# The second layer's modulation sums, divided between the context feed-forward and the first latent feed-forward

## The chip, the cores and the metric

One core of a Trainium2 chip runs the whole program. The time is the device time of one execution in microseconds; the profile is one further execution of the same program, recorded by the hardware profiler. TensorE does matrix products, VectorE, ScalarE and GpSimd the rest, and SyncE issues transfers between HBM and SBUF; each engine works through its own queue in order.

## The reference

A transformer of two layers with width 1024 works on 1024 latent tokens `x` and 256 context tokens `ctx`, in fp32. The first layer mixes by recurrences, the second by attention; both end in a gated feed-forward with a convolution over three tokens. Each layer has six modulation vectors (`_ada`), for the latent tokens from the condition `c` and for the context tokens from `c_ctx`.

```python
def _rms(x):
    xf = x.astype(jnp.float32)
    return (xf * lax.rsqrt(jnp.mean(xf * xf, axis=-1, keepdims=True) + EPS)).astype(x.dtype)

def _modulate(h, shift, scale):
    return h * (1.0 + scale) + shift

def _ada(cond, w, b):
    m = (jax.nn.silu(cond) @ w + b)[:, None, :]
    return jnp.split(m, 6, axis=-1)

def _conv_ffn(h, w_up, conv_w, w_down):
    gate, val = jnp.split(h @ w_up, 2, axis=-1)
    gate = _dwconv(gate, conv_w)
    return (jax.nn.silu(gate) * val) @ w_down

    for i in range(DEPTH):
        last = i == DEPTH - 1
        ml = _ada(c, mod_w[i], mod_b[i])
        mc = _ada(c_ctx[None], mod_w[i], mod_b[i])
        h_l = _modulate(_rms(x), ml[0], ml[1])
        h_c = _modulate(_rms(ctx), mc[0], mc[1])
        ...
        x = x + ml[2] * mix_l
        x = x + ml[5] * _conv_ffn(_modulate(_rms(x), ml[3], ml[4]), ffn_w_up[i], ffn_conv[i], ffn_w_down[i])
        if not last:
            ctx = ctx + mc[2] * mix_c
            ctx = ctx + mc[5] * _conv_ffn(_modulate(_rms(ctx), mc[3], mc[4]), ffn_w_up[i], ffn_conv[i], ffn_w_down[i])
    return _rms(x) * final_norm
```

In the attention of the second layer, queries and keys are normalised by `_rms` over their 128 channels, multiplied by a gain and, for latent tokens, rotated.

## The kernel before

The stages follow each other in this order in the span: recurrences (to about 940 us), output projection of the recurrent mixer (to 1117), feed-forward of the context tokens (`ffn_ctx`, to 1400), feed-forward of the latent tokens in the first layer (`ffn_run(0, ...)`, to about 2070), queries, keys and values of the second layer (to about 2300), attention, the second layer's latent feed-forward (`ffn_run(1, ...)`), the last normalisation. The program is written stage by stage, with generators that mix work of one stage into another; a scheduler that runs when the program is built then fixes the order of the instructions on every engine from its own estimate of times. A tile pool with so many buffers limits how far a load can run ahead of its use.

**Modulation sums.** `mod_steps` computes one part of a modulation vector. For each of 8 blocks of 128 rows of `mod_w` it loads a tile `mw`, and VectorE adds `mw` times a scalar per partition to `macc` (`ts` for the first, L98, `stt` for the others, L103). Then TensorE sums `macc` over the partitions (`mps`, L229), and VectorE adds the bias (`mod<-mps,modb`). For the second layer (l = 1) all six indices are worked on in the context stage, in pieces of 512 columns with two `mw` buffers: 12 pieces x 8 = 96 loads of 256 KB, asked for with `next(mods)` five times per hidden block f, on SyncE's queue. Indices 0 and 1 are needed for both conditions (`macc0`, `macc1`), the others for the latent tokens alone.

**Context stage.** `ffn_ctx` goes over NF = 22 hidden blocks of 128 channels. `up_mm` multiplies with fp32 weights (`fg<-hx,st`, L1203, 256 tokens wide), and after every four blocks `downs` adds to `xT[0]` (`fd<-ft,st`, L1212). Weights come in tiles `st` of 256 KB on the same queue. Beside it `ffn_prep` normalises the latent tokens for the next stage, in 8 pieces of 128 tokens (`rm_ps`: two matmuls a piece, L173 and L180, with a power on GpSimd between them, `rm_cs`). At the end the context tokens are normalised and modulated for the second layer and written to `x0_scr`.

**Latent stage.** `ffn_run` goes over the same 22 blocks. `up(f)` loads 512 KB of weights twice, splits them into a high and a low part (ScalarE copies, GpSimd or VectorE subtracts: `w0h`, `w0l`, `s0h`, ...) and multiplies three times (`mm3`, L155 to L157), in a scheme that needs seven products instead of eight (`u`, `fraw`, `p` are its sums; `st<-st` are sums of weights). `silu_conv` forms the gate on `ft`, and `gated` splits the result into `gh` and `gl`. After every two blocks `downs` multiplies with the down weights (`dh`, `dl`, loads `sd` of 128 KB) into `fd`, and VectorE adds to `xT`. Pools here: `wd` (4 buffers), `g` (2), `st` (2), `w` (1), `t` (1).

**Norm and rope.** `norm_rope` in the stage of queries, keys and values squares (`qsq`, ScalarE), sums (`qss`, VectorE), takes the power (`qrs`, GpSimd), multiplies (`qn`, VectorE) and rotates.

Of the kernel before, what the change touches and what calls it, by code (L numbers as in the profile page):

```python
# [70 lines left out]
def kernel(  # L71
# [139 lines left out]
    def mod_steps(pool, psp, tag, l, idx, conds, part, width, bufs=2):  # L211
# [13 lines left out]
        for d in conds:  # L225
            ps = psp.tile([128, 512], F32, tag=tag, name="mps")
            w_ = 128 if width < 512 else 1
            for m in range(nm):
                T.matmul(ps[:, m * w_:m * w_ + w_], lhsT=acc[d][:, m * 128:(m + 1) * 128], rhs=ones[:, 0:w_],  # L229
                         start=True, stop=True)  # L230
            j0 = c0 // 128
            m_ = modc[l][d][:, j0:j0 + nm]
            tt(V, m_, ps[:, 0:nm * w_].rearrange("p (m n) -> p m n", n=w_)[:, :, 0:1].rearrange("p m n -> p (m n)"),
               modb[:, l * 48 + j0:l * 48 + j0 + nm], ALU.add)
            if idx in (1, 4):
                ts(V, m_, m_, 1.0, None, ALU.add)
            if idx == 5:
                ts(V, m_, m_, 0.5, None, ALU.mult)
# [213 lines left out]
    eG = const.tile([128, NB, 8], F32, name="eG")  # L452
    nG = const.tile([128, NB, 8], F32, name="nG")
    eT = const.tile([128, NB, 8], F32, name="eT")
    ekc = const.tile([128, NB, 8], F32, name="ekc")
    rq2 = const.tile([128, 4, NB], F32, name="rq2")
    rqs = const.tile([128, 4, NB], F32, name="rqs")
# [1176 lines left out]
```

## Time and profile before

| | |
|---|---|
| median of 3 runs (lowest, highest) | 3442.43 us (3440.96, 3444.37) |
| profiled execution: time, span | 3442.76 us, 3441.0 us |
| mean granted TensorE clock | 0.962 |
| busy: TensorE, VectorE | 3195.9 us (93%), 2402.4 us (70%) |
| busy: GpSimd, ScalarE | 1436.7 us (42%), 1278.5 us (37%) |
| moved by DMA | 350.10 MB, mean 102 GB/s |

The span goes from the first to the last instruction; the time of the execution has 1.76 us around it. Shares of busy time are averages over stages with different limits, so single stages are read from windows, waits and timelines below.

### The profile page before, as it was taken

How to read it: one execution, taken by the hardware profiler on the slowest of the kernel's cores; microseconds unless marked ns; L12 is line 12 of the kernel's file. 1: busy time of each engine (PE TensorE's matmuls, PEld its weight loads, DVE VectorE, ACT ScalarE, POOL GpSimd, SP SyncE). 2: the span in 40 equal slices, each digit the busy share in tenths (PEclk: the TensorE clock that was granted, in tenths of full speed). 3: DMA queues.
4: the chain of work that ended last, by engine and by line, in shares of the span. 5: the costliest groups of instructions: out<-in, count | busy, mean ns of one | idle time of the engine just before them, and what ended most of it. 6: DMA issues, size and time to landing. Idle time of an engine off the chain costs nothing.

```text
span 3441.0 us, 47011 instructions
## 1 busy us (share of the span) xinstructions
PE 3195.9 (93%) x16708; PEld 2666.6 (77%) x16708; DVE 2402.4 (70%) x4108; ACT 1278.5 (37%) x2772; POOL 1436.7 (42%) x1269
## 2 busy tenths in 40 slices
PE   7987988999979998899999997999999799999998
PEld 4776877777768887778788786988888678887877
DVE  5567467568777866676777768677567767777677
ACT  4434233653321212333333333346556433333333
POOL 2232231233214111465565553753433655655554
PEclk9998999999989999899999998999999899999999
DMA  5445444655586677212111111330111111111111
GB/s 185 117 117 164 134 133 130 180 152 163 185 263 187 195 231 213 71 52 59 49 55 44 52 57 51 112 99 32 44 47 31 32 53 52 55 45 52 58 50 71
DMA packets 439241, 350.10 MB, mean 102 GB/s; under 512 B 55989, under 2 KB 379807, under 8 KB 438239
## 3 DMA queue, kind: packets, MB, share of 16 engines
q1 hardware_dynamic: 439006, 347.10, 34.0%
q8 instruction: 132, 2.16, 0.3%
q14 instruction: 103, 0.84, 0.1%
HBM read 286.25 MB, written 60.76 MB: 101 GB/s over the span
## 4 chain that ended last, share of the span: by engine, by line
PE 44%; DVE 7%; POOL 3%; issue 2%; ACT 2%; DMA 0%; DVEq 0%; POOLq 0%; ACTq 0%
PE fg L157 6%; PE fg L155 6%; PE fg L156 6%; PE fd L156 4%; PE fd L157 4%; PE fd L155 4%; PE apo L155 2%; PE apo L157 2%; PE apo L156 2%; DVE st L94 2%; PE apt L1512 2%; POOL w1l L94 1%; PE s L155 1%; PE qps L157 1%; PE qps L156 1%
## 5 line engine op out<-in xcount | busy, mean ns | idle before, releaser
L103 DVE SCALAR_TENSOR_TENSOR xT<-fd,mod,xT 128x512 f32<-128x512 f32 (+1 forms) x432 | 290.9, 694 | 193.8 <-PE fd L157 174.0
L155 PE MATMUL pj<-hhi,whi 128*128 128x512 f32 (+1 forms) x696 | 263.8, 379 | 21.3 <-ACT raw L510 14.7
L156 PE MATMUL fd<-gl,dh 128*128 128x512 f32 (+1 forms) x688 | 267.8, 389 | 6.7 <-DVE gl L94 6.6
L157 PE MATMUL fd<-gh,dl 128*128 128x512 f32 (+1 forms) x688 | 266.8, 388 | 0.0
L155 PE MATMUL fd<-gh,dh 128*128 128x512 f32 (+1 forms) x688 | 262.6, 392 | 1.0 <-ACT gh L1140 0.7
L156 PE MATMUL pj<-hlo,whi 128*128 128x512 f32 (+1 forms) x696 | 261.0, 375 | 1.2 <-DVE hlo L94 1.2
L157 PE MATMUL pj<-hhi,wlo 128*128 128x512 f32 (+1 forms) x696 | 259.7, 373 | 0.0
L94 DVE TENSOR_TENSOR st<-st 128x512 f32<-128x512 f32 x176 | 211.6, 1203 | 48.7 <-POOL s1l L94 35.6
L103 DVE SCALAR_TENSOR_TENSOR macc<-mw,sc,macc 128x512 f32<-128x512 f32 (+2 forms) x210 | 177.4, 873 | 82.4 <-DMA mw<-in_mod_w_dram 81.4
L94 POOL TENSOR_TENSOR dl<-sd,dh 128x256 fp32r<-128x256 f32 x168 | 156.1, 944 | 107.4 <-ACT dh L160 107.4
L100 POOL TENSOR_SCALAR P<-P,rc 128x512 f32<-128x512 f32 (+1 forms) x192 | 116.2, 622 | 199.3 <-DVE rc L1498 64.1
L94 POOL TENSOR_TENSOR wlo<-wst,whi 128x512 fp32r<-128x512 f32 x58 | 77.4, 1336 | 271.0 <-ACT whi L160 270.7
L94 POOL TENSOR_TENSOR w0l<-st,w0h 128x1024 fp32r<-128x1024 f32 x44 | 106.0, 2410 | 189.5 <-ACT w0h L1085 134.9
L155 PEld LDWEIGHTS pj<-hhi,whi 128*128 128x128 f32 x696 | 138.3, 199 | 45.9 <-ACT raw L510 17.0
L1203 PE MATMUL fg<-hx,st 128*128 128x256 f32 x704 | 168.5, 393 | 4.3 <-DMA st<-in_ffn_w_up_dram 3.6
L156 PEld LDWEIGHTS fd<-gl,dh 128*128 128x128 f32 x688 | 130.0, 189 | 39.3 <-DVE gl L94 12.8
L94 POOL TENSOR_TENSOR p<-p,u 128x512 f32<-128x512 f32 (+1 forms) x45 | 94.2, 2094 | 149.6 <-DVE u L94 149.6
L103 DVE SCALAR_TENSOR_TENSOR ft<-fraw,conv_f,ft 128x1024 f32<-128x1024 f32 x88 | 135.6, 1541 | 29.2 <-ACT ft L91 28.4
L155 PEld LDWEIGHTS fd<-gh,dh 128*128 128x128 f32 x688 | 128.1, 188 | 35.4 <-ACT gh L1140 9.9
L1203 PEld LDWEIGHTS fg<-hx,st 128*128 128x128 f32 x704 | 136.2, 197 | 24.7 <-DMA st<-in_ffn_w_up_dram 2.1
L156 PEld LDWEIGHTS pj<-hlo,whi 128*128 128x128 f32 x696 | 138.3, 199 | 19.5 <-DVE hlo L94 1.4
L157 PEld LDWEIGHTS pj<-hhi,wlo 128*128 128x128 f32 x696 | 138.0, 198 | 18.9 <-issue 0.2
(609 smaller groups left out, 9697.5 us busy)
## 6 DMA issues: line engine op xcount, KB each, us to landing
st<-in_ffn_w_up_dram SPq DMA_DIRECT2D x88, 512.0 KB
mw<-in_mod_w_dram SPq DMA_DIRECT2D x96, 256.0 KB
st<-in_ffn_w_up_dram SPq DMA_DIRECT2D x88, 256.0 KB
sd<-in_ffn_w_down_dram SPq DMA_DIRECT2D x176, 128.0 KB
sh<-sh_scr SPq DMA_DIRECT2D x80, 256.0 KB
wst<-in_rec_w_in_dram SPq DMA_DIRECT2D x56, 256.0 KB
st<-in_rec_w_out_dram SPq DMA_DIRECT2D x24, 512.0 KB
mw<-in_mod_w_dram SPq DMA_DIRECT2D x24, 512.0 KB
```

The source lines that it names most:

```text
L94: e.tensor_tensor(out=o, in0=a, in1=b, op=op)
L100: e.tensor_scalar(out=o, in0=a, scalar1=s1, scalar2=s2, op0=op0, op1=op1)
L103: e.scalar_tensor_tensor(out=o, in0=a, scalar=s, in1=b, op0=op0, op1=op1)
L155: T.matmul(ps, lhsT=wh, rhs=xh, start=first, stop=False)
L156: T.matmul(ps, lhsT=wh, rhs=xl, start=False, stop=False)
L157: T.matmul(ps, lhsT=wl, rhs=xh, start=False, stop=last)
L1203: T.matmul(ps, lhsT=h[k // 4][:, k % 4], rhs=hx[:, k], start=k == 0, stop=k == KD - 1)
L1512: T.transpose(pt_[:, b], P[:, (b0 + b) * 128:(b0 + b + 1) * 128], ident)
```

## The change

The sums of the second layer are divided. Indices 1, 0 and 2 stay in the context stage, now in pieces of 256 columns, loaded by GpSimd's queue into six buffers; `mod_chain` puts the end of a piece (`fin`: matmuls on `macc` and the addition of the bias) two steps into the next piece, and `fill` is called within `ffn_ctx` at the places where weights are loaded. Indices 4, 3 and 5 move into the first latent feed-forward, in pieces of 256 columns on SyncE's queue with two buffers, by `fill` in `ffn_run`.

Buffers change places: some small tables lie in a pool on the right side that is closed after the recurrences; the latent stage's pools `st`, `w` and `t` lie on the right and are opened before the context tokens' last normalisation; that normalisation (`ctx_out`) becomes a hook after `up(0)` of the latent stage; `wd` gets three buffers instead of four, and the last block's down weights go into the tiles `s0` and `s1`; `fsta` has 11 buffers instead of 12.

In `norm_rope` the sum of squares is taken by ScalarE itself (`accum_out`), and the product `qn` moves from VectorE to ScalarE.

```diff
+    pa = ExitStack()
+    rcs = pool(pa, "rcs", 1, side="right")
...
+    def mod_steps(pool, psp, tag, l, idx, conds, part, width, bufs=2, eng=None, late=None):
...
-        acc = {d: pool.tile([128, width], F32, tag=f"macc{d}", name="macc") for d in conds}
+        acc = {d: pool.tile([128, width], F32, tag=f"macc{d}", name="macc", bufs=1 if late is None else 2) for d in conds}
...
-            dma(w, mod_w[l, k * 128:(k + 1) * 128, c0:c0 + width])
+            (eng or nc.sync).dma_start(out=w, in_=mod_w[l, k * 128:(k + 1) * 128, c0:c0 + width])
...
+    def mod_chain(specs):
+        late = []
+        for sp in specs:
+            for i, _ in enumerate(mod_steps(*sp, late=late)):
+                if i == 1 and len(late) > 0:
+                    late.pop(0)()
+                yield
+        for fin in late:
+            fin()
...
-    def ffn_run(l, p, ops, early):
+    def ffn_run(l, p, ops, early, hook=None, fill=lambda: None):
...
                 for ci in (1, 2):
                     for k in (kp, kp + 1):
                         down(fs, hs, k, ci, 0, 512)
+                    fill()
...
             t1 = up(f)
+            if f == 0 and hook is not None:
+                hook()
...
             gated(f, t1)
-        w1 = [w_part(f, kp) for kp in range(0, KD, 2)]
+            fill()
+        if l == 0:
+            w1 = []
+            for e in range(2):
+                big = hilo(p.w, [128, 4, 128], f"s{e}")
+                w1 += [w_part(f, 4 * e + kp, [u[:, kp:kp + 2] for u in big]) for kp in (0, 2)]
+        else:
+            w1 = [w_part(f, kp) for kp in range(0, KD, 2)]
...
                 h = [weight(w_down(0, f), hf) for f in fs]
+                fill()
...
             pg = up_mm(w_up(0, f * 128))
             if f % GRP_F == 0 and f:
                 downs(range(f - GRP_F, f))
+            fill()
             pv_ = up_mm(w_up(0, DFF + f * 128))
+            fill()
...
-            mods = (None for i in (1, 0, 2, 4, 3, 5) for h in range(2)
-                    for _ in mod_steps(mp, pd, "d", 1, i, (0, 1) if i < 2 else (0,), h, 512))
+            mods = mod_chain([(mp, pd, "d", 1, i, (0, 1) if i < 2 else (0,), q, 256, 6, nc.gpsimd) for i in (1, 0, 2) for q in range(4)])
...
-                for _ in range(5):
-                    next(mods, None)
+                next(mods, None)
+                next(mods, None)
...
-            hx = hilo(h0, [128, KD, NCTX], "m0")
-            rms_mod(tmp, pd, "d", xT[0], NCTX, mcol(1, 1, 1), mcol(1, 1, 0), *hx, w=128)
-            for i in range(2):
-                dma(x0_scr[i], hx[i])
-    with ExitStack() as pf:
-        p = Ffn()
-        ffn_pools(p, 0, pf, (("wd", 4), ("g", 2), ("st", 2), ("w", 1), ("t", 1)))
-        ffn_run(0, p, ops, 0)
+        h0s.close()
+    pf = ExitStack()
+    p = Ffn()
+    x0p = pool(p0, "x0p", 1)
+    for nm, b in (("st", 2), ("w", 1), ("t", 1)):
+        setattr(p, nm, pool(pf, f"f{nm}0", b, side="right"))
+
+    def ctx_out():
+        for o in range(0, NCTX, 128):
+            xs = xT[0][:, :, o:o + 128]
+            rb, sq = normalised(x0p, pd, "d", xs)
+            tt(V, sq, xs, rb, ALU.mult)
+            scale_shift(sq, sq, mcol(1, 1, 1), mcol(1, 1, 0))
+            hi = x0p.tile([128, KD, 128], F32R, tag="xhi", name="xhi")
+            lo = sq.bitcast(F32R)
+            for k in (0, 4):
+                S.copy(out=hi[:, k:k + 4], in_=sq[:, k:k + 4])
+                tt(V, lo[:, k:k + 4], sq[:, k:k + 4], hi[:, k:k + 4].bitcast(F32), ALU.subtract)
+            dma(x0_scr[0][:, :, o:o + 128], hi)
+            dma(x0_scr[1][:, :, o:o + 128], lo)
+        p0.close()
+        p.wd = pool(pw, "fwd0", 3)
+        p.g = pool(pw, "fg0", 2)
+        mq.append(pool(pw, "fm0", 1))
+
+    with ExitStack() as pw:
+        mq = []
+        mods = mod_chain([(mq, pd, "d", 1, i, (0,), q, 256) for i in (4, 3, 5) for q in range(4)])
+        ffn_run(0, p, ops, 0, ctx_out, lambda: next(mods, None))
...
             def norm_rope(ps, b, a):
                 sq = qt_.tile([128, 2, 128], F32, tag="sq", name="qsq")
-                act(sq, ps, AF.Square)
-                ss = qt_.tile([128, 2], F32, tag="ss", name="qss")
-                V.tensor_reduce(out=ss, in_=sq, axis=AX.X, op=ALU.add)
...
+                for h in range(2):
+                    S.activation(out=sq[:, h], in_=ps[:, h], func=AF.Square, accum_out=ss[:, 0, h:h + 1])
...
-                tt(V, qn, ps, rs[:, :, None].to_broadcast([128, 2, 128]), ALU.mult)
+                for h in range(2):
+                    act(qn[:, h], ps[:, h], AF.Copy, scale=ss[:, 1, h:h + 1])
```

The scheduler's order shows how the instructions move. The first place is GpSimd's queue at the start of the context stage, before the change; `wol` are the last splits of the output projection's weights, and `rm_cs` is the power on which TensorE's `rm_ps` waits.

```order
L94 TENSOR_TENSOR wol<-st,woh 128x1024 x13
L176 TENSOR_TENSOR rm_cs<-rm_cs,nhalf 128x1 x2
L94 TENSOR_TENSOR wol<-st,woh 128x1024
L100 TENSOR_SCALAR hx<-rm_sq,mod_72 128x128 x4
L94 TENSOR_TENSOR wol<-st,woh 128x1024 x2
L176 TENSOR_TENSOR rm_cs<-rm_cs,nhalf 128x1
L100 TENSOR_SCALAR rm_sq<-rm_sq,mod_71 128x128 x2
```

The same place in GpSimd's queue after the change, from the last two `wol` on:

```order
L94 TENSOR_TENSOR wol<-st,woh 128x1024 x2
L221 DMA mw<-in_mod_w_dram 128x256 x22
L178 TENSOR_TENSOR rm_cs<-rm_cs,nhalf 128x1
L100 TENSOR_SCALAR rm_sq<-rm_sq,mod_74 128x128 x2
L221 DMA mw<-in_mod_w_dram 128x256
L178 TENSOR_TENSOR rm_cs<-rm_cs,nhalf 128x1
L221 DMA mw<-in_mod_w_dram 128x256 x7
L100 TENSOR_SCALAR rm_sq<-rm_sq,mod_74 128x128 x2
```

The loads of `mw` have come into this queue, in runs of up to 22 ahead of a power. The second place is TensorE's queue where the context stage (`fd` from `ft` and fp32 weights `st`) ends and the latent stage (`fg` from `ah`, `al` and split weights `w0h`, `w0l`) begins, before the change:

```order
L1212 MATMUL fd<-ft_11844,st 128x256
L1212 MATMUL fd<-ft_11878,st 128x256
L1212 MATMUL fd<-ft_11844,st 128x256
L1212 MATMUL fd<-ft_11878,st 128x256
L173 MATMUL rm_ps<-ones,rm_rs 128x128
L155 MATMUL fg<-ah,w0h 128x512
L156 MATMUL fg<-al,w0h 128x512
L155 MATMUL fg<-ah,w0h 128x512
L156 MATMUL fg<-al,w0h 128x512
L173 MATMUL rm_ps<-ones,rm_rs 128x128
```

The same boundary after the change:

```order
L1241 MATMUL fd<-ft_11852,st 128x256
L1241 MATMUL fd<-ft_11898,st 128x256
L1241 MATMUL fd<-ft_11852,st 128x256
L1241 MATMUL fd<-ft_11898,st 128x256
L157 MATMUL fg<-ah,w0h 128x512
L158 MATMUL fg<-al,w0h 128x512
L157 MATMUL fg<-ah,w0h 128x512
L158 MATMUL fg<-al,w0h 128x512
L159 MATMUL fg<-ah,w0l 128x512
```

The context tokens' normalisation (`rm_ps`) no longer stands between the two stages; it comes some 20 rows later. The third place is VectorE's queue within one block f of the latent stage, before the change: the chain on `ft_14075` from the convolution to `gl`, with what stands between its steps (`st<-st` are sums of the next block's weights).

```order
L103 SCALAR_TENSOR_TENSOR ft_14075<-fraw,conv_f,ft_14075 128x1024 x2
L94 TENSOR_TENSOR u_14077<-fg,u_14077 128x512
L94 TENSOR_TENSOR st<-st 128x512
L103 SCALAR_TENSOR_TENSOR ft_14075<-fraw,ft_14075 128x1024
L94 TENSOR_TENSOR st<-st 128x512
L94 TENSOR_TENSOR ft_14075<-u_14077,ft_14075 128x2x256
L94 TENSOR_TENSOR st<-st 128x512
L94 TENSOR_TENSOR gl<-ft_14075,gh 128x512 x2
```

Such a chain after the change, on `ft_14255`:

```order
L103 SCALAR_TENSOR_TENSOR ft_14255<-fraw,conv_f,ft_14255 128x1024
L103 SCALAR_TENSOR_TENSOR macc<-mw,sc,macc 128x256
L103 SCALAR_TENSOR_TENSOR ft_14255<-fraw,conv_f,ft_14255 128x1024
L103 SCALAR_TENSOR_TENSOR macc<-mw,sc,macc 128x256 x2
L103 SCALAR_TENSOR_TENSOR ft_14255<-fraw,ft_14255 128x1024
L103 SCALAR_TENSOR_TENSOR macc<-mw,sc,macc 128x256
L94 TENSOR_TENSOR ft_14255<-u_14257,ft_14255 128x2x256
L103 SCALAR_TENSOR_TENSOR macc<-mw,sc,macc 128x256
L94 TENSOR_TENSOR u_14412<-fg,fraw 128x512
L103 SCALAR_TENSOR_TENSOR macc<-mw,sc,macc 128x256
L94 TENSOR_TENSOR fraw<-fg,fraw 128x2x256
L94 TENSOR_TENSOR gl<-ft_14255,gh 128x512 x2
```

Six `macc` stand there between the chain's steps, and no `st<-st`.

## Rows read from the trace of the kernel before

**Rows 1.** Windows: stretch, then busy us (instructions) by engine, granted clock, DMA share, GB/s.

```profile
1130.00:1350.00 220.00, 210.61 (x997) 181.67 (x997) 162.99 (x298) 48.94 (x98) 27.66 (x32) 0.97 0.74 217
1376.00:1400.00 24.00, 23.82 (x97) 20.16 (x96) 7.74 (x18) 0.00 (x0) 0.00 (x0) 0.88 0.00 0
1404.82:2068.00 663.18, 652.70 (x2820) 529.53 (x2821) 475.26 (x524) 216.63 (x360) 386.72 (x271) 0.99 0.19 57
```

**Rows 2.** TensorE's timeline, context stage: start us, us, work, [idle before].

```profile
1117.32 0.46 PE L1203 MATMUL fg<-hx,st 128*128 128x256 f32 x1
...
1288.23 0.38 PE L173 MATMUL rm_ps<-ones,rm_rs 128*128 128x128 f32 x2
1288.45 2.32 PE L1203 MATMUL fg<-hx,st 128*128 128x256 f32 x10
1290.62 0.95 PE L229 MATMUL mps<-ones,macc 128*128 128x1 f32 x8
1291.43 1.54 PE L1203 MATMUL fg<-hx,st 128*128 128x256 f32 x6
...
1341.16 9.23 PE L1203 MATMUL fg<-hx,st 128*128 128x256 f32 x42
...
1375.91 23.91 PE L1212 MATMUL fd<-ft,st 128*128 128x256 f32 x96
...
1404.82 0.80 PE L155 MATMUL fg<-ah,w0h 128*128 128x512 f32 x1 [0.60 <-ACT w0h L1085]
```

**Rows 3.** Groups of TensorE, 1121 to 1400 us: busy, mean ns, idle before.

```profile
L1203 PE MATMUL fg<-hx,st 128*128 128x256 f32 x689 | 165.2, 393 | 4.3 <-DMA st<-in_ffn_w_up_dram 3.6 <-ACT rm_sq L91 0.6
L1212 PE MATMUL fd<-ft,st 128*128 128x256 f32 x352 | 84.5, 393 | 2.1 <-DVE xT L103 2.0
L229 PE MATMUL mps<-ones,macc 128*128 128x1 f32 x128 | 17.0, 257 | 13.2 <-DVE macc L103 12.9 <-DVE xT L103 0.4
```

**Rows 4.** Groups of VectorE, 1121 to 1400 us.

```profile
L103 DVE SCALAR_TENSOR_TENSOR macc<-mw,sc,macc 128x512 f32<-128x512 f32 x100 | 75.6, 770 | 52.1 <-DMA mw<-in_mod_w_dram 51.7
L103 DVE SCALAR_TENSOR_TENSOR xT<-fd,mod,xT 128x256 f32<-128x256 f32 x48 | 22.6, 478 | 19.5 <-PE fd L1212 19.5
...
L98 DVE TENSOR_SCALAR macc<-mw,sc 128x512 f32<-128x512 f32 x14 | 6.7, 477 | 0.0
```

**Rows 5.** SyncE's queue, loads issued: start us, us, transfer.

```profile
1364.54 0.33 SPq L84 DMA_DIRECT2D mw<-in_mod_w_dram  x1
...
1399.42 1.00 SPq L84 DMA_DIRECT2D st<-in_ffn_w_up_dram  x2
```

**Rows 6.** TensorE's waits, 1376 to 1450 us: total, times, longest.

```profile
PE fg L155 <- ACT s1h L1094: 2.0, 1, 2.0
PE fg L157 <- POOL s3l L94: 1.4, 1, 1.4
```

**Rows 7.** TensorE's waits, 1450 to 2068 us.

```profile
PE fd L156 <- DVE gl L94: 3.4, 9, 0.4
```

**Rows 8.** Groups of GpSimd, 940 to 1400 us.

```profile
L94 POOL TENSOR_TENSOR wol<-st,woh 128x1024 fp32r<-128x1024 f32 x16 | 42.0, 2630 | 80.3 <-ACT woh L160 80.3
...
L176 POOL TENSOR_TENSOR rm_cs<-rm_cs,nhalf 128x1 f32<-128x1 f32 x10 | 6.7, 672 | 147.3 <-DVE rm_cs L100 147.3
```

**Rows 9.** Groups of VectorE, 1450 to 2068 us.

```profile
L94 DVE TENSOR_TENSOR st<-st 128x512 f32<-128x512 f32 x80 | 97.0, 1212 | 21.4 <-POOL s1l L94 16.0 <-POOL w1l L94 5.3
```

**Rows 10.** Groups of VectorE, 2080 to 2290 us.

```profile
L94 DVE TENSOR_TENSOR qn<-qps,qrs 128x256 f32<-128x256 f32 x42 | 17.6, 419 | 3.0 <-POOL qrs L1413 2.3
L1410 DVE TENSOR_REDUCE qss<-qsq 128x2 f32<-128x256 f32 x42 | 17.4, 414 | 16.3 <-ACT qsq L91 16.0
```

**Rows 11.** Groups of ScalarE, 2080 to 2290 us.

```profile
L91 ACT ACTIVATE qsq<-qps 128x256 f32<-128x256 f32 x42 | 16.2, 387 | 65.1 <-DVE qn L94 25.2 <-PE qps L157 23.9 <-POOL qrs L1413 4.8
```

**Rows 12.** TensorE's waits, 2070 to 2300 us.

```profile
PE qtr L1447 <- DVE qn L94: 1.7, 3, 1.1
```

**Rows 13.** TensorE's waits, 940 to 1117 us.

```profile
PE po L1289 <- DMA st<-in_rec_w_out_dram: 9.6, 3, 5.4
```

More of the change, by code (lines that the diff above doesn't have):

```diff
@@ L224, in mod_steps, with fin @@
             yield
[L225 to L238, printed above, removed]
+        def fin():
+            for d in conds:
+                ps = psp.tile([128, 512], F32, tag=tag, name="mps")
+                w_ = 128 if width < 512 else 1
+                for m in range(nm):
+                    T.matmul(ps[:, m * w_:m * w_ + w_], lhsT=acc[d][:, m * 128:(m + 1) * 128], rhs=ones[:, 0:w_],
+                             start=True, stop=True)
+                j0 = c0 // 128
+                m_ = modc[l][d][:, j0:j0 + nm]
+                tt(V, m_, ps[:, 0:nm * w_].rearrange("p (m n) -> p m n", n=w_)[:, :, 0:1].rearrange("p m n -> p (m n)"),
+                   modb[:, l * 48 + j0:l * 48 + j0 + nm], ALU.add)
+                if idx in (1, 4):
+                    ts(V, m_, m_, 1.0, None, ALU.add)
+                if idx == 5:
+                    ts(V, m_, m_, 0.5, None, ALU.mult)
+        if late is None:
+            fin()
+        else:
+            late.append(fin)
+    def mod_chain(specs):
[6 more added lines that the diff above has]
+        for fin in late:
+            fin()
     def mod_acc(*a):
@@ L450, in dn_run @@
                 dn_step(h, d, n)
[L452 to L457, printed above, removed]
+    eG = rcs.tile([128, NB, 8], F32, name="eG")
+    nG = rcs.tile([128, NB, 8], F32, name="nG")
+    eT = rcs.tile([128, NB, 8], F32, name="eT")
+    ekc = rcs.tile([128, NB, 8], F32, name="ekc")
+    rq2 = rcs.tile([128, 4, NB], F32, name="rq2")
+    rqs = rcs.tile([128, 4, NB], F32, name="rqs")
     pieces = [(2, q4) for q4 in range(4)]
@@ L1235 @@
     KORD = (4, 1, 5, 0, 2, 7, 6, 3)
-    with ExitStack() as p0:
+    p0 = ExitStack()
+    h0s = ExitStack()
+    if True:
         fa, fc = Ffn(), Ffn()
@@ L1308 @@
         with ExitStack() as pf:
[L1309 removed]
+            fa.st = pool(pf, "fsta", 11)
             mp = pool(pf, "mpa", 1)
[L1311 to L1312 removed]
+            mods = mod_chain([(mp, pd, "d", 1, i, (0, 1) if i < 2 else (0,), q, 256, 6, nc.gpsimd) for i in (1, 0, 2) for q in range(4)])
             fa.g = pool(pf, "fga", 6)
             fa.t = pool(pf, "fta", 2)
[L1315 removed]
+            step = ffn_ctx(fa, hx, lambda: next(mods, None))
             tmp = pool(pf, "tmpa", 1)
@@ L1327 @@
             dump("xf0_0", xT[0])
-            hx = hilo(h0, [128, KD, NCTX], "m0")
-            rms_mod(tmp, pd, "d", xT[0], NCTX, mcol(1, 1, 1), mcol(1, 1, 0), *hx, w=128)
-            for i in range(2):
-                dma(x0_scr[i], hx[i])
-    with ExitStack() as pf:
-        p = Ffn()
-        ffn_pools(p, 0, pf, (("wd", 4), ("g", 2), ("st", 2), ("w", 1), ("t", 1)))
-        ffn_run(0, p, ops, 0)
+        h0s.close()
[25 more added lines that the diff above has]
+        ffn_run(0, p, ops, 0, ctx_out, lambda: next(mods, None))
+        for _ in mods:
+            pass
         for ci in (1, 2):
             dump(f"xf0_{ci}", xT[ci])
+    pf.close()
     hEs.close()
```

24 lines of the change are left out of this document (12 added, 12 removed).

## The prediction

> **What bounds the kernel now.** I read the windows first, to see which engine sets the pace in the stages that the change touches. In the context feed-forward TensorE is busy 210.6 of 220 us between 1130 and 1350 us, at a mean granted clock of 0.97, and the transfers are dense there (share 0.74); in the first latent feed-forward, from 1404.82 us on, it is busy 652.7 of 663.2 us, with VectorE at 475.3 us and transfers at 0.19 [rows 1]. So TensorE bounds both, and what counts is where it stands idle or runs at less than full clock.
>
> How much of the context stage is more than its matrix work is read from TensorE's timeline. The stage runs from 1117.32 to 1375.91 + 23.91 = 1399.82 us, 282.5 us [rows 2]. One undisturbed run of 42 records takes 9.23 us, the last record's own 0.39 among it: (9.23 - 0.39) / 41 = 0.2156 us a record [rows 2]. (A matmul in fp32 leaves two records.) The stage has 22 hidden blocks x 2 x 8 x 2 = 704 records of the up projection and 22 x 8 x 2 = 352 of the down projection; the group rows hold 689 and 352, the first 15 lie ahead of their window [rows 3]. That is 1056 x 0.2156 = 227.7 us. The reduction of the modulation sums (mps) comes in groups of 8 records, 0.81 us from one start to the next work's start (1290.62 to 1291.43); its 128 records make 16 groups, 13.0 us [rows 2, 3]. The normalisations' matmuls cost 0.22 us per two (1288.23 to 1288.45), 32 of them, 3.5 us [rows 2]. Together 244.2 us, so **38.3 us of the stage are lost**. The groups name two causes: mps waited 12.9 us for macc, and the up projection 3.6 us for its weights [rows 3]. Why macc is late is seen on VectorE: its sums sat 51.7 us waiting for mw [rows 4]. In SyncE's queue an mw load stands among the weight loads [rows 5], with two buffers. The rest of the loss is restarts and clock: the last 96 records, back to back with no transfer, took 23.91 us at a clock of 0.88 [rows 1, 2] instead of 96 x 0.2156 = 20.7.
>
> Between 1399.82 and 1404.82 us TensorE does little but the normalisation ahead of the next stage, whose first weights are issued only at 1399.42 us [rows 2, 5]; then it waits another 2.0 and 1.4 us for split weights [rows 6]. After that the latent stage hardly waits: 9 times on gl, 3.4 us in all [rows 7].
>
> **The change, part by part.**
>
> *Context stage: -29.7 us.* Gone are the 16 mps groups of 0.81 us. In their place stand 4 pieces x (2 + 2 + 1) sums = 20 sets of two matmuls with 128 columns; priced by the normalisation's 0.22 us per two records that is 0.44 us a set, 8.8 us. The matrix work becomes 227.7 + 8.8 + 3.5 = 240.0 us. The order shows the last macc now far ahead of the last down projection, and SyncE's queue holds no mw in this stage; mw's bytes halve. VectorE's work hardly changes: 160 operations with 256 columns (0.478 us for the same operation on xT) are 76 us, against some 114 macc of 0.770 and 0.477 us, 82 us, in the window [rows 4]. How much of the 38.3 us comes back no row tells: at least the 12.9 us of macc, at most all. Since the weight wait of 3.6 us and the restarts have other causes too, but fewer transfers ease both, I let a third stay, 12.8 us: a stage of 252.8 us, 29.7 us shorter.
>
> *Loads by GpSimd's queue.* The trace has no load issued there. From below, SyncE issues one in 0.33 us [rows 5]; from above, the longest operation on GpSimd lasts 2.63 us, a small one 0.67 [rows 8]. I take 1 us: 96 loads are 96 us beside about 28 us of other work on this engine [rows 1], hidden in 253 us. Queued behind a load that waits for one of six buffers are GpSimd's powers (rm_cs), and behind these TensorE's rm_ps; that costs nothing while loads take about this long. The loads themselves, 128 KB, have six buffers of lead.
>
> The Trainium skill, page "SBUF — State Buffer", section "SBUF: two separate sides", speaks against this edit: GpSimd writes the descriptors of its loads itself and is shut out while VectorE runs an operation that takes both ports. No run here has shown it. By that rule each first macc of a piece, if its fast form is such an operation, would hold the queue: 20 x 0.48 = 10 us of an engine with some 130 us to spare, no change in the sum.
>
> *Boundary: -5 us, and -3 us behind it.* The first latent weights are loaded and split during the last context blocks, the normalisation stands behind the first up projection, and the order shows the fg rows directly after fd. The gap of 5.0 us goes (bounds 0 and 5.0); of 3.4 us of waits for splits [rows 6] I take 3 (bounds 0 and 3.4). What is late next is the second up projection's weights, which w's single buffer still holds back as before.
>
> *First latent feed-forward: +5.3 and +8 us.* 12 pieces x 0.44 = 5.3 us on TensorE. On VectorE 96 x 0.478 = 45.9 us come in, 475.3 + 45.9 = 521 of 663 us, 79%: room on average. But gl was just on time [rows 7], and macc now stands in its chain. What the order shows is an exchange: before, three st sums of 1.21 us [rows 9] stood in one chain, 3.6 us; now six macc, 2.9 us, and the st go elsewhere. So the chain need not grow. Against it: 96 loads come back into SyncE's queue with two buffers, so a weight load can stand behind an mw that waits for VectorE; and wd has three buffers instead of four. Bounds 0 and 45.9 us (every macc on the path); I take 8, near the lower end because of the exchange.
>
> *Norm and rope: -2 us.* VectorE loses a reduction of 0.414 and a product of 0.419 us in each of 42 places, 35 us [rows 10]; ScalarE gets two squares for one and two copies, at most 3 x 0.387 us more [rows 11], 49 us on an engine with over half of the stage free. TensorE waited 1.7 us for qn here [rows 12]. Bounds: -4 and, if ScalarE's chain is the longer one, +4.
>
> *Other places.* The pools on the right side move no work; the output projection's loads may shift against its wait of 9.6 us [rows 13]. I take 0, bounds -5 and +5.
>
> Sum: -29.7 - 5.0 - 3.0 + 5.3 + 8.0 - 2.0 = -26.4 us. The profiled run took 3442.76 us (span 3441.0 and 1.76 around it), so 3416.4; the median of the runs shown lies 0.3 us lower: **3416 us**.
>
> **The rivals.** By 0.2%, about what a measurement of this kernel can tell from no change, faster is below 3435.5 and slower above 3449.3 us.
>
> (a) *The latent stage pays it back.* macc in the gl chain makes fd wait. All 45.9 us on the path instead of 8: 3416 + 37.9 = **3454 us**, slower. It is level from (3435.5 - 3416 + 8) / 45.9 = 60% of macc's time on the path and slower from 90%. For it: gl had no slack, 79% of VectorE, two buffers. Against it: the exchange above, and TensorE's order there is rearranged with up projections between shorter blocks of down projections. 0.15 (0.09 level, 0.06 slower).
>
> (b) *GpSimd's queue is the new bound.* The stage becomes 28 + 96 x t. At 2.63 us a load it is 280 us, and the kernel 3444; slower from 2.69 us; with SyncE's 0.33 on top (2.96 us), 312 us and **3475 us**. For it: no row shows such a load, and rm_ps stands behind them on TensorE. Against it: only the widest operations on GpSimd last so long. 0.09, nearly all slower. The Trainium skill, page "SBUF — State Buffer", gives it a mechanism by the section named above.
>
> (c) *Nothing is lost any more.* The stage takes its 240.0 us and macc in the latent stage costs nothing: -42.5 - 5 - 3 + 5.3 - 2 = -47.2, **3395 us**. For it: the latent stage's full clock shows that TensorE can run so; against it: weight loads of 256 KB still come at a high rate. 0.14.
>
> (d) *The sums were only part of the loss.* Nothing but macc's 12.9 us comes back; 25.4 us stay, a stage of 265.4 us, 12.6 more than in my sum: **3429 us**. For it: only a third of the 38.3 us has macc's name. Against it: the clock falls after the waits. 0.16.
>
> **How the numbers follow.** My forecast has 0.46, with a range of its own from 3405 to 3425 (8 either way for the context third, 8 for the latent stage below). Faster: 0.46 + 0.14 + 0.16 = 0.76; level 0.09 from (a) and 0.01 from (b); slower 0.06 + 0.08 = 0.14. The range takes in (d), the level part of (a) and most of (c): 3388 to 3442 leaves out the slower cases and the end of (c), under 0.2.
>
> **What the changed profile would show.** Right: no wait of mps for macc in the context stage, which lasts about 253 us at a clock near 1; fg follows fd within 1 us at the boundary; fd's waits for gl in the latent stage under 10 us. Wrong: GpSimd busy through the whole context stage and rm_ps waiting for it (b); fd waiting for gl, or for dl and dh behind SyncE's mw, over 25 us (a); fg waiting for st as before (d).

## The result, and the profile after

The changed kernel takes 3467.0 us in the median (3463.0 to 3473.6, 4 runs) against 3441.7 us for the kernel before on the same chip: a ratio of 1.0074, with a 95% interval from 1.0062 to 1.0087. It is slower, by 25 us, where the prediction had 3416 us. The profiled execution has a span of 3471.8 us, 30.8 more than before; it is the longest of the four, and the four lie 10.6 us apart, so the stages below add up to 30.8 us and not to 25.

The stages were measured on TensorE's timeline, from a stage's first record to the end of its last one. For the changed kernel, the context stage begins, its last down projections begin, and the latent stage begins with these rows:

```profile
1119.24 2.26 PE L1231 MATMUL fg<-hx,st 128*128 128x256 f32 x7
...
1354.53 7.07 PE L1241 MATMUL fd<-ft,st 128*128 128x256 f32 x32
1362.30 0.50 PE L157 MATMUL fg<-ah,w0h 128*128 128x512 f32 x1 [0.70 <-ACT w0h L1103]
```

The latent stage ends at 2122.3 us. Set against before:

| us | before | changed | difference |
|---|---|---|---|
| context stage (first `fg<-hx` to last `fd<-ft`) | 282.5 | 242.4 | -40.1 |
| from there to the first latent `fg` | 5.0 | 0.7 | -4.3 |
| latent stage (to the last `fd<-gh`) | 695.5 | 760.0 | +64.5 |
| from there to the first `qps` | 0.8 | 5.2 | +4.4 |
| queries, keys and values | 182.5 | 180.4 | -2.1 |
| second layer's latent feed-forward | 724.6 | 730.5 | +5.9 |
| everything else | 1550.1 | 1552.6 | +2.5 |

So the context stage gained more than was predicted, and the latent stage lost all of it and 24 us more. The windows of the changed kernel that answer to [rows 1] (stretch, busy us by engine TensorE, its weight loads, VectorE, ScalarE, GpSimd, then granted clock, DMA share, GB/s):

```profile
1130.00:1350.00 220.00, 220.00 (x1073) 195.08 (x1072) 156.18 (x351) 52.21 (x106) 71.64 (x109) 1.00 0.64 191
1362.30:2122.30 760.00, 704.10 (x3010) 567.07 (x3011) 556.82 (x677) 226.69 (x368) 365.89 (x270) 0.96 0.23 68
```

In the context stage TensorE is busy in all of 220 us at full clock. In the latent stage it is idle for 56 of 760 us at a mean clock of 0.96; before, over the whole stage, it was 0.99 and 17 of 695:

```profile
1404.82:2100.27 695.45, 678.00 (x2960) 550.34 (x2961) 503.68 (x562) 222.87 (x366) 388.00 (x272) 0.99 0.19 56
```

So some 38 of the 64.5 us are idle time, and 26 us are more busy time: the sums' own matmuls, matmuls at the lower clock, and matmuls that take longer at full clock (e11 below).

The groups of TensorE in the context stage answer to [rows 3], where the last number, the idle time ahead of them, is now zero in all three:

```profile
L1231 PE MATMUL fg<-hx,st 128*128 128x256 f32 x704 | 159.8, 382 | 0.0
L1241 PE MATMUL fd<-ft,st 128*128 128x256 f32 x352 | 79.2, 379 | 0.0
L234 PE MATMUL mps<-ones,macc 128*128 128x128 f32 (+1 forms) x84 | 11.8, 274 | 0.0
```

GpSimd's queue issues a load like this (start us, us; the wait in brackets is for a free buffer):

```profile
1146.80 0.54 POOL L221 DMA_DIRECT2D mw<-in_mod_w_dram  x1 [0.28 <-DVE macc L103]
1147.59 0.54 POOL L221 DMA_DIRECT2D mw<-in_mod_w_dram  x1 [0.26 <-DVE macc L103]
```

What TensorE waits for in the latent stage (total us, times, longest) has changed altogether from [rows 7]:

```profile
PE fg L157 <- ACT fraw L1138: 24.6, 8, 3.9
PE fd L157 <- DVE xT L103: 10.2, 7, 2.5
PE fg L157 <- ACT s0h L1112: 7.5, 2, 4.5
PE fd L157 <- ACT gh L1158: 5.8, 1, 5.8
```

The chief wait is not on `gl`. It is `fg`, the sixth product of an up projection: five PSUM buffers hold the products, so the sixth needs the one that ScalarE empties by copying the first product into `fraw`. How one such wait of 2.2 us arises is seen on VectorE's timeline of one block:

```profile
1688.18 0.69 DVE L94 TENSOR_TENSOR st<-st 128x512 f32<-128x512 f32 x1 [2.43 <-POOL s1l L94]
...
1689.45 0.68 DVE L94 TENSOR_TENSOR gl<-ft,gh 128x512 fp32r<-128x512 f32 x1
...
1690.80 1.77 DVE L94 TENSOR_TENSOR gl<-ft,gh 128x512 fp32r<-128x512 f32 x1
1692.50 0.47 DVE L103 SCALAR_TENSOR_TENSOR macc<-mw,sc,macc 128x256 f32<-128x256 f32 x1
1693.80 1.28 DVE L103 SCALAR_TENSOR_TENSOR ft<-fraw,conv_f,ft 128x1024 f32<-128x1024 f32 x1 [0.83 <-ACT ft L91]
1695.00 2.63 DVE L103 SCALAR_TENSOR_TENSOR macc<-mw,sc,macc 128x256 f32<-128x256 f32 x1
1697.55 1.27 DVE L103 SCALAR_TENSOR_TENSOR ft<-fraw,conv_f,ft 128x1024 f32<-128x1024 f32 x1
1698.75 0.47 DVE L103 SCALAR_TENSOR_TENSOR macc<-mw,sc,macc 128x256 f32<-128x256 f32 x1
1699.72 0.48 DVE L103 SCALAR_TENSOR_TENSOR macc<-mw,sc,macc 128x256 f32<-128x256 f32 x1 [0.49 <-DMA mw<-in_mod_w_dram]
1700.12 1.22 DVE L103 SCALAR_TENSOR_TENSOR ft<-fraw,ft 128x1024 f32<-128x1024 f32 x1
```

The same moment on GpSimd (`w0l`), ScalarE (the copy to `fraw`) and TensorE:

```profile
1694.79 2.56 POOL L94 TENSOR_TENSOR w0l<-st,w0h 128x1024 fp32r<-128x1024 f32 x1 [2.76 <-ACT w0h L1103]
...
1701.37 0.59 ACT L1138 COPY fraw<-fg 128x512 f32<-128x512 f32 x1 [1.39 <-DVE ft L103]
...
1702.01 0.50 PE L157 MATMUL fg<-t2h,s2h 128*128 128x512 f32 x1 [2.19 <-ACT fraw L1138]
```

Read from the top: a sum of weights (`st`) stands ahead of `gl` and had to wait 2.43 us for GpSimd's split. `gl` comes late, and with it the next `ft`, whose single buffer `gl` still reads. Then macc stands between the steps of the chain on `ft`: one takes 2.63 us, and another waits 0.49 us for its load. The chain reads `fraw` until 1701.3 us; only then can ScalarE write the next block's first product there (1701.37), and only then does TensorE go on (1702.01). VectorE's waits add up to this in the stage:

```profile
DVE st L94 <- POOL s1l L94: 31.5, 14, 3.2
...
DVE macc L103 <- DMA mw<-in_mod_w_dram: 29.8, 31, 3.4
```

### The profile page after: what moved, and what is told of

The parts are those of the page before. It is cut to its first block, busy times and chain, and to the rows that moved or that the text cites. A ratio compares the mean times of both kernels' runs of the same rounds, so it can differ in the third digit from the quotient of the medians.

```text
span 3471.8 us, 47446 instructions
## 1 busy us (share of the span) xinstructions
PE 3199.7 (92%) x16708; PEld 2665.3 (77%) x16708; DVE 2400.4 (69%) x4177; ACT 1309.1 (38%) x2982; POOL 1466.6 (42%) x1363
## 4 chain that ended last, share of the span: by engine, by line
PE 63%; DVE 17%; DMA 7%; ACT 4%; POOL 4%; issue 3%; SPq 1%; DVEq 0%; ACTq 0%; POOLq 0%
PE fg L157 6%; PE fg L159 6%; PE fg L158 5%; PE fg L1231 4%; PE fd L158 4%; PE fd L159 4%; PE fd L157 4%; PE fd L1241 2%; PE apo L157 2%; PE apo L159 2%; PE apo L158 2%; PE pj L157 2%; DVE ft L103 2%; DVE st L94 2%; PE apt L1569 2%
## 5 line engine op out<-in xcount | busy, mean ns | idle before, releaser
L158 PE MATMUL fd<-gl,dh 128*128 128x512 f32 (+1 forms) x664 | 259.1, 390 | 3.1 <-DVE gl L94 3.1
L159 PE MATMUL fd<-gh,dl 128*128 128x512 f32 (+1 forms) x664 | 255.1, 390 | 1.1 <-POOL dl L94 1.1
L103 DVE SCALAR_TENSOR_TENSOR macc<-mw,sc,macc 128x256 f32<-128x256 f32 (+1 forms) x322 | 212.5, 691 | 51.8 <-DMA mw<-in_mod_w_dram 50.5
L94 DVE TENSOR_TENSOR st<-st 128x512 f32<-128x512 f32 x176 | 196.0, 1115 | 74.1 <-POOL s1l L94 51.4
L94 POOL TENSOR_TENSOR dl<-sd,dh 128x256 fp32r<-128x256 f32 x164 | 149.1, 923 | 71.7 <-ACT dh L162 71.1
L1231 PE MATMUL fg<-hx,st 128*128 128x256 f32 x704 | 159.8, 382 | 0.0
L94 POOL TENSOR_TENSOR p<-p,u 128x512 f32<-128x512 f32 (+1 forms) x45 | 76.3, 1696 | 185.3 <-DVE u L94 164.7
L157 PE MATMUL fg<-ah,w0h 128*128 128x512 f32 (+1 forms) x360 | 141.6, 394 | 6.9 <-ACT ah L1047 6.2
```

Source lines behind the costliest of these rows:

```text
L94: e.tensor_tensor(out=o, in0=a, in1=b, op=op)
L103: e.scalar_tensor_tensor(out=o, in0=a, scalar=s, in1=b, op0=op0, op1=op1)
L157: T.matmul(ps, lhsT=wh, rhs=xh, start=first, stop=False)
L158: T.matmul(ps, lhsT=wh, rhs=xl, start=False, stop=False)
L159: T.matmul(ps, lhsT=wl, rhs=xh, start=False, stop=last)
L1231: T.matmul(ps, lhsT=h[k // 4][:, k % 4], rhs=hx[:, k], start=k == 0, stop=k == KD - 1)
```

## The experiments

Three theories for the latent stage's 64.5 us. **A**: the sums' work on VectorE stands in the chain. **B**: macc waits there for its loads. **C**: the buffer places, three `wd` buffers above all, make the stage slow by themselves. The table has the stages that the runs gave (us), with their ratio to the kernel before on the same chip where it was timed. Each stage is read from one profiled execution; e4, whose latent stage has the order of before on every engine, shows that 1.5 us there can come with no change.

| kernel | context | latent | ratio (95% interval) |
|---|---|---|---|
| before | 282.5 | 695.5 | |
| changed | 242.4 | 760.0 | 1.0074 (1.0062 to 1.0087) |
| e1, no latent sums | 242.4 | 725.9 | 0.9953 (0.9939 to 0.9967) |
| e2, one load per piece | 242.3 | 735.0 | one run |
| e3, all sums in context | 259.3 | 729.1 | 1.0020 (1.0011 to 1.0029) |
| e4, norm and rope alone | 280.7 | 694.0 | 1.0002 (0.9992 to 1.0012) |
| e5, e1 with four `wd` and the old end | 240.7 | 700.3 | one run |
| e6, e1 with four `wd` | 240.7 | 697.6 | one run |
| e7, e3 with four `wd` and the old end | 259.4 | 699.8 | 0.9945 (0.9931 to 0.9959) |
| e8, before with GpSimd's queue | 260.1 | 694.4 | 0.9929 (0.9915 to 0.9943) |
| e9, divided, four `wd` | 242.4 | 742.5 | 1.0027 (1.0012 to 1.0043) |
| e10, latent loads by GpSimd | 242.4 | 752.2 | one run |
| e11, e8 with the tables right | 258.7 | 705.8 | 0.9975 (0.9963 to 0.9986) |

**e1: without the latent stage's sums.** They are left out, with a constant in their place.

```diff
+    V.memset(modc[1][0][:, 24:48], 0.5)
-        ffn_run(0, p, ops, 0, ctx_out, lambda: next(mods, None))
-        for _ in mods:
-            pass
+        ffn_run(0, p, ops, 0, ctx_out)
```

> Changed kernel without the sums of indices 4, 3 and 5 in the first latent feed-forward (they are left out, a constant stands in their place); all buffer places, three wd buffers and the context stage as changed. The latent stage (first fg to last fd) took 695.5 us before and 760.0 changed. Theory A (the sums' work on VectorE stands in the silu chain) and theory B (macc waits there for mw loads in SyncE's queue) both expect about 695 to 705 us and a kernel of about 3405 us. Theory C (the buffer places, three wd buffers above all, and the order built around them make the stage slow by themselves) expects 740 us or more and a kernel of about 3450 us.

Measured: 725.9 us. 34.1 us of the 64.5 go with the sums, 30.4 stay without any. That is between the theories (705 and 740). So A or B has a part, and C as well. Two waits that led to `fraw` in the changed kernel stand in e1 without any macc, between 1400 and 2040 us:

```profile
DVE st L94 <- POOL s1l L94: 38.4, 19, 3.2
...
PE fg L158 <- ACT fraw L1139: 17.0, 8, 2.5
```

**e2: one load for eight macc.**

```diff
-            w = pool.tile([128, width], F32, tag="mw", name="mw", bufs=bufs)
-            (eng or nc.sync).dma_start(out=w, in_=mod_w[l, k * 128:(k + 1) * 128, c0:c0 + width])
+            if k == 0 or l == 0 or eng is not None:
+                w = pool.tile([128, width], F32, tag="mw", name="mw", bufs=bufs)
+                (eng or nc.sync).dma_start(out=w, in_=mod_w[l, k * 128:(k + 1) * 128, c0:c0 + width])
```

> Changed kernel whose sums in the latent stage load mw once per piece and use it eight times: 12 loads instead of 96, the same 96 macc operations on VectorE (the sums themselves are wrong, as seven of eight row blocks are left out). Theory A: the latent stage stays near 750 us, macc at about 0.73 us each. Theory B: macc no longer waits for mw, and the stage falls to 710 to 725 us. Theory C: as A, 745 us or more.

Measured: 735.0 us, which lies outside what each theory expected (A 750, B 710 to 725, C 745 or more). Against e1 the work costs 9.1 us (5.3 of it would be TensorE's own reduction, by the prediction's price), and the 84 loads more cost 25.0. Of the sums' part B is the larger.

**e3: all sums in the context stage, the places as changed.**

```diff
-... 256, 6, nc.gpsimd) for i in (1, 0, 2) for q in range(4)])
+... 256, 6, nc.gpsimd) for i in (1, 0, 2, 4, 3, 5) for q in range(4)])
-                next(mods, None)
-                next(mods, None)
+                for _ in range(7):
+                    next(mods, None)
```

(and `ffn_run` without `fill`, as in e1)

> Changed kernel with all six indices in the context stage, 192 loads of 128 KB on GpSimd's queue and seven requests per block there, none in the latent stage; buffer places as changed. The context stage (242.4 us changed, 282.5 before) grows by 12 more sets of two matmuls, 5.3 us, to 248 us if GpSimd's queue and VectorE keep up; if VectorE becomes its bound (256 macc of 0.48 us and about 95 us of other work are 218 us), it stays under 260 us. Theories A and B: latent stage about 700 us, kernel about 3410 us. Theory C: latent stage 740 us, kernel about 3455 us.

Measured: context 259.3 us, 16.9 more than changed, where 5.3 of TensorE's work were added; the latent stage 729.1 us, between the theories (700 and 740) and again 33.6 too long without sums (C). To do three indices' sums in the context stage costs 17 us, in the latent stage 34.

**e4: norm and rope alone**, on the kernel before.

```diff
+            ts(V, nb_, nb_, 128 ** 0.5, None, ALU.mult)
-                act(sq, ps, AF.Square)
+                for h in range(2):
+                    S.activation(out=sq[:, h], in_=ps[:, h], func=AF.Square, accum_out=ss[:, 0, h:h + 1])
```

(and the rest of `norm_rope` as in the change)

> Kernel before with the change of norm and rope alone. Forecast of the prediction: 2 us faster, at most 4 faster or 4 slower; the stage of queries, keys and values took 182.5 us before and 180.4 changed. The rival, that the 4.5 us longer gap ahead of that stage and the later stages come from norm and rope, expects the kernel 5 to 10 us slower here.

Measured: 182.2 us in its stage (182.5 before) and a ratio of 1.0002. The stage shows 0.3 us; the ratio's interval, from 2.8 us faster to 4.1 slower, can't tell the forecast 2 us from nothing. The rival of 5 to 10 us falls: the gap ahead of the stage and the second feed-forward (725.5 us) are those of before.

**e5: e1 with four `wd` buffers and the last weights in `wd`.**

```diff
-        p.wd = pool(pw, "fwd0", 3)
+        p.wd = pool(pw, "fwd0", 4)
-        if l == 0:
-            w1 = []
-            for e in range(2):
-                big = hilo(p.w, [128, 4, 128], f"s{e}")
-                w1 += [w_part(f, 4 * e + kp, [u[:, kp:kp + 2] for u in big]) for kp in (0, 2)]
-        else:
-            w1 = [w_part(f, kp) for kp in range(0, KD, 2)]
+        w1 = [w_part(f, kp) for kp in range(0, KD, 2)]
```

> As e1 (sums of indices 4, 3 and 5 left out of the latent stage), with four wd buffers and the last block's down weights in wd as before. Latent stage 725.9 us in e1, 695.5 before. Theory C1 (the third of wd's buffers taken away, with the tail that goes with it, makes the 30.4 us): 695 to 700 us. Theory C2 (the hook, the pools on the right side or the early first splits make them): 715 us or more.

Measured: 700.3 us, 25.6 less than e1: C1 holds, and 4.8 us are left to C2. (In these 4.8 us TensorE is idle no longer than before, 17 to 18 us in both; it is busy 4.5 us longer.) In the same stretch `st` waits half as long, TensorE no longer waits for `fraw`, and most of its waiting is again that on `gl`, at most 0.4 us at a time, as in [rows 7]:

```profile
DVE st L94 <- POOL s1l L94: 19.6, 12, 2.1
...
PE fd L159 <- DVE gl L94: 3.0, 8, 0.4
```

What the scheduler wrote differs too. With four buffers the order is nearly that of before: where down projections stand between the steps of a block's chain, the last nine operations of VectorE ahead of `gl` are all on `xT` (9 of 22 blocks before, 8 in e5). With three, `gl` of 8 blocks comes after the next block's first sums, with four `st` among the last eight operations ahead of it. The count shows directly too. `dh` lies in these buffers, and ScalarE can write the next one only when `fd` has read an old one; e1 first, then e5, 1400 to 2040 us:

```profile
ACT dh L163 <- PE fd L159: 70.7, 36, 10.6
```

```profile
ACT dh L163 <- PE fd L159: 44.2, 13, 7.0
```

How much of the 25.6 us is this wait on ScalarE, ahead of the next splits, and how much the order, wasn't separated.

**e6: e5 with the last weights in `s0` and `s1`** (only the line of `wd` is changed against e1).

> As e5, but the last block's down weights stay in the tiles s0 and s1. From the second last block on the latent stage took 94.5 us before and 107.6 in e1. If the tiles s0 and s1 make these 13 us, the latent stage is 708 to 712 us and that end 106 to 108; if the three buffers make them, it is that of e5 and the end 95 us.

Measured: 697.6 us, and 94.9 us from the second last block on, the 94.9 of e5. The tiles cost nothing that shows; the 13 us at the end came from the three buffers too.

**e7: e3 with four `wd` buffers and the old end**, nothing left out.

> As e3 (all six indices in the context stage by GpSimd's queue, nothing left out), with four wd buffers and the old end of the latent stage. By C1: context stage 259 us as in e3, latent stage 695 to 700, so about 24 us less than the kernel before (ratio about 0.993). By C2: latent stage 715 us or more, and about the time of before.

Measured: 259.4 and 699.8 us, ratio 0.9945. C1 again: 29.3 us against e3. The gain is 19 us, not 24, since the gap ahead of the next stage (7.5 us) and the second feed-forward (729.0) keep their losses.

**e8: the kernel before, with the sums by GpSimd's queue.** All six indices stay in the context stage; places, hook and norm are those of before.

```diff
-            fa.st = pool(pf, "fsta", 12)
+            fa.st = pool(pf, "fsta", 11)
-            mods = (None for i in (1, 0, 2, 4, 3, 5) for h in range(2)
-                    for _ in mod_steps(mp, pd, "d", 1, i, (0, 1) if i < 2 else (0,), h, 512))
+            mods = mod_chain([(mp, pd, "d", 1, i, (0, 1) if i < 2 else (0,), q, 256, 6, nc.gpsimd) for i in (1, 0, 2, 4, 3, 5) for q in range(4)])
-                for _ in range(5):
+                for _ in range(7):
                     next(mods, None)
```

(and `mod_steps`, `mod_chain` and the `fill` of `ffn_ctx` as in the change)

> Kernel before with one part of the change alone: the six sums stay in the context stage, but by 192 loads of 128 KB on GpSimd's queue, six buffers, ends of pieces put late (fsta 11); buffer places, hook, latent stage and norm as before. Theory: the queue and the late ends alone give the context stage's gain; 282.5 us becomes about 259, latent stage 695.5, ratio about 0.993. Rival: the gain needs fewer sums in the stage or the early latent loads; context stage over 272 us, ratio 0.997 or more.

Measured: 260.1 and 694.4 us, a ratio of 0.9929 (0.9915 to 0.9943), some 24 us faster than before: with e7, whose interval overlaps its own, the fastest version here that leaves nothing out. The queue with its six buffers, the narrower pieces and the late ends together, without any of the moves to other places, take 22.4 us from the context stage; they weren't tried singly. TensorE's groups there, as in [rows 3]: 3.6 us of waiting for macc and 1.3 for weights are left.

```profile
L1220 PE MATMUL fg<-hx,st 128*128 128x256 f32 x704 | 164.5, 383 | 3.0 <-ACT ft L91 1.7 <-DMA st<-in_ffn_w_up_dram 1.3
L1230 PE MATMUL fd<-ft,st 128*128 128x256 f32 x352 | 81.5, 383 | 0.8 <-DVE xT L103 0.7
L232 PE MATMUL mps<-ones,macc 128*128 128x128 f32 (+1 forms) x135 | 20.7, 280 | 3.7 <-DVE macc L103 3.6 <-DVE xT L103 0.2
```

**e9: divided, with four `wd` buffers.**

```diff
-        p.wd = pool(pw, "fwd0", 3)
+        p.wd = pool(pw, "fwd0", 4)
-        mods = mod_chain([(mq, pd, "d", 1, i, (0,), q, 256) for i in (4, 3, 5) for q in range(4)])
-        ffn_run(0, p, ops, 0, ctx_out, lambda: next(mods, None))
+        mods = mod_chain([(mq, pd, "d", 1, i, (0,), q, 128) for i in (4, 3, 5) for q in range(8)])
+        ffn_run(0, p, ops, 0, ctx_out, lambda: (next(mods, None), next(mods, None)))
```

(and the old end, as in e5)

> Changed kernel with four wd buffers and the old end of the latent stage; so that this fits, the sums in the latent stage work in pieces of 128 columns (192 loads of 64 KB on SyncE's queue, two buffers, two requests per place); nothing is left out. With the buffers right (700 us in e5) the division itself is priced: by the difference of the changed kernel to e1 (760.0 - 725.9 = 34 us) the latent stage is 730 to 740 us, the kernel about 3442, no faster than before and slower than e8. If the sums hurt only together with three buffers, the latent stage is 705 to 715 us and the kernel about 3417.

Measured: 742.5 us, 42.2 more than e5 (730 to 740 us was expected), and a ratio of 1.0027. So the division costs with four buffers too, and the sums don't hurt only together with three. That the two losses simply add up isn't shown: here the loads are twice as many and half as large, macc waits longer for them, 67.7 us in place of 29.8, and TensorE waits elsewhere, for `xT` and no longer for `fraw`:

```profile
DVE macc L103 <- DMA mw<-in_mod_w_dram: 67.7, 58, 5.4
...
PE fd L157 <- DVE xT L103: 19.8, 26, 2.5
```

**e10: the latent stage's loads by GpSimd's queue.**

```diff
-        mods = mod_chain([(mq, pd, "d", 1, i, (0,), q, 256) for i in (4, 3, 5) for q in range(4)])
+        mods = mod_chain([(mq, pd, "d", 1, i, (0,), q, 256, 2, nc.gpsimd) for i in (4, 3, 5) for q in range(4)])
```

> Changed kernel whose sums in the latent stage load mw by GpSimd's queue, still with two buffers; SyncE's queue holds only weights there. The loads cost 25 us of the latent stage (760.0 us, against 735.0 with 12 loads in e2). If they cost it because weight loads queue behind mw on SyncE, the stage falls to 735 to 742 us. If they cost it because macc waits for its own load, with two buffers and some 3.6 us from issue to landing, it stays at 755 us or more, and GpSimd's splits come later besides.

Measured: 752.2 us, 7.8 less than changed; 735 to 742 was expected if SyncE's order were the cause, 755 or more if it were macc's own wait. It lies nearer to the second, and macc waited 38.3 us, more than the 29.8 on SyncE's queue. So SyncE's order may have a small part; most of the loads' price stays when they leave that queue. In part this run pays a price of its own: 96 issues of 0.54 us take some 52 us of GpSimd's time. But the weights tell the same: ScalarE's first split of a block waited no longer for its weights in the changed kernel than before (below, before and then changed, 1400 to 2040 us), which speaks against mw holding them up on SyncE's queue.

```profile
DVE macc L103 <- DMA mw<-in_mod_w_dram: 38.3, 26, 4.8
```

```profile
ACT w0h L1085 <- DMA st<-in_ffn_w_up_dram: 51.9, 17, 3.8
```

```profile
ACT w0h L1103 <- DMA st<-in_ffn_w_up_dram: 40.9, 16, 3.7
```

**e11: e8 with the small tables on the right side** (pool `rcs`, as in the change).

```diff
+    pa = ExitStack()
+    rcs = pool(pa, "rcs", 1, side="right")
-    conv_r = const.tile([128, 36], F32, name="conv_r")
+    conv_r = rcs.tile([128, 36], F32, name="conv_r")
```

(and so for the other tables)

> As e8, with one more part of the change: the small tables (conv_r, b2c, nrmc, eG and others) in the pool rcs on the right side, which moves the addresses of what is allocated later. TensorE's order of the second latent feed-forward is the same before and changed, yet its blocks 3 to 20 took 548.5 us before, 545.8 in e8 and 552 to 553 in all kernels with the new places. If the addresses set this, e11 takes 552 us there and the kernel some 4 to 8 us more than e8; if not, 546 to 549 us and e8's time.

Measured: blocks 3 to 20 of the second feed-forward take 552.2 us (545.8 in e8), the first latent stage 705.8 (694.4), the ratio is 0.9975 instead of 0.9929. The place of a few small tables costs some 12 us, more than the 4 to 8 expected. Not all of the 6.4 us in blocks 3 to 20 is longer work: TensorE's order there differs between e8 and e11, and the whole second feed-forward takes 728.9 against 725.3 us. TensorE waits for nothing new in it; single matmuls are longer. Two groups of e8, then the same of e11 (busy, mean ns), 2760 to 3240 us:

```profile
L157 PE MATMUL fg<-bh,s3l 128*128 128x512 f32 x64 | 24.9, 389 | 0.0
L155 PE MATMUL fg<-t3h,w1h 128*128 128x512 f32 x64 | 24.9, 389 | 0.0
```

```profile
L159 PE MATMUL fg<-bh,s3l 128*128 128x512 f32 x64 | 25.3, 395 | 0.0
L157 PE MATMUL fg<-t3h,w1h 128*128 128x512 f32 x64 | 25.3, 395 | 0.0
```

389 ns become 395 at a granted clock of 1.00 in both. A cleaner comparison is e11 with the kernel before. In the first latent stage TensorE and VectorE have the same instructions in the same order in both, yet e11 takes 705.8 us and the kernel before 695.5. TensorE's busy time tells where they go, 689.70 us (below) against the 678.00 of before, at a clock of 0.99 in both; it is idle no longer.

```profile
1384.71:2090.49 705.78, 689.70 (x2962) 550.00 (x2962) 504.63 (x562) 222.83 (x366) 387.40 (x272) 0.99 0.19 55
```

So neither order nor waits make the difference. What moved for these matmuls is the address of their operands, and that it is the cause follows from what is left; which addresses are slow, and why, was not tried.

## Why the prediction was wrong

- **Context stage, -29.7 us: right in kind, too small.** It gained 40.1. The matrix work was 240.0 us by the sum, the stage takes 242.4: instead of the third of the loss that I let stay, 2.4 us stayed. The clock's part went with the waits, as rival (c) had it for this stage, and (d) fell.
- **GpSimd's queue, 1 us a load: 0.54 us.** All 96 loads of the changed kernel lie between 0.536 and 0.758 us. Rival (b) fell. The Trainium skill, page "SBUF — State Buffer", section "SBUF: two separate sides", has such loads held up while VectorE runs an operation in a mode that takes both ports. The median of 0.536 us, beside a VectorE that is busy 156 of 220 us, shows no sign of it; whether VectorE ran such an operation here, the trace does not tell.
- **Boundary, -5 us: -4.3.** The 3 us behind it did not come: the next waits for splits (`s0h`, 7.5 us) took their place.
- **Norm and rope, -2 us: -0.3 us in the stage alone** (e4; too small for its ratio to tell).
- **First latent feed-forward, +13.3 us: +64.5. This is the step that failed**, in three terms. Even its upper bound, 5.3 + 45.9 = 51.2 us, was too low, since it counted macc's own time alone.
  1. "wd has three buffers instead of four" was named and given no price. It costs 25.6 us (e1 against e5) to 29.3 (e3 against e7). With it come an order in which `st` sums that wait for GpSimd stand ahead of `gl`, and a ScalarE that waits 36 times instead of 13 for a free `dh`; the share of each is open. The order shown ahead of the prediction had it: the `st` that left the chain of one block did not vanish. I counted them as an exchange and didn't ask where they went.
  2. The sums' loads cost 25.0 us (changed against e2). I knew the two buffers and put them into a single remark; macc's wait for its own load stood in the context stage's rows already (51.7 us, [rows 4]), and the change carried that wait with it to the stage that hardly waited.
  3. The sums' work costs 9.1 us (e2 against e1), near the 5.3 on TensorE. But macc was priced from `xT<-fd`, 0.478 us [rows 4], one of whose inputs lies in PSUM. In the latent stage, where GpSimd is busy, it took 0.728 and 0.920 us in the mean, 72 us instead of 45.9:

```profile
L103 DVE SCALAR_TENSOR_TENSOR macc<-mw,sc,macc 128x256 f32<-128x256 f32 x84 | 61.2, 728 | 30.4 <-DMA mw<-in_mod_w_dram 29.8
...
L98 DVE TENSOR_SCALAR macc<-mw,sc 128x256 f32<-128x256 f32 x12 | 11.0, 920 | 1.8 <-DMA mw<-in_mod_w_dram 1.8
```

  With the 4.8 us that e5 is longer than before these are 25.6 + 25.0 + 9.1 + 4.8 = 64.5. The four are steps of one chain of kernels, so they must add up; in another sequence the shares could differ (29.3 for the first, 42.2 for the sums in e9). The 4.8 are longer matmuls, as in e11, more than waits, but hook, pools and tables weren't tried one by one there.
- **The signs of being right came true** all the same: no wait of mps for macc (0.0 us), a context stage at a clock of 1.00, `fg` 0.7 us after `fd`, no wait of `fd` for `gl`. They watched what had been slow before, and none of them looked at `fraw`, so they could not tell right from wrong.
- **Rival (a)** named the stage and the sign. Its 45.9 us for the sums compare with 34.1 measured (e1); its place, `fd` waiting for `gl`, was wrong: TensorE waited for `fraw`, one step further on.
- **Addresses** were counted at nothing ("move no work"). The second feed-forward's 5.9 us have the same order of TensorE's instructions as before; e11 loses 4.3 us there and 10.3 us in the first latent stage with the tables' pool alone.

Left open: what of three buffers is the count and what the order; whether more `mw` buffers in the latent stage would take away the loads' 25.0 us, which no run tried; why the gap ahead of queries, keys and values grows from 0.8 to 5.2 us (it is 5 to 7.5 in every kernel with the hook and the right-side pools, and 0.8 in e4, e8 and e11); which addresses slow a matmul.
